# A two-layer diffusion backbone: another order of its stages, and norm gains applied where rows are loaded

## The chip, the cores and the metric

The kernel runs on one core of one Trainium2 chip. The metric is the device time of one execution, in microseconds (us); less is better. The engines of the core are TensorE (PE in the profile; PEld is its weight load), VectorE (DVE), ScalarE (ACT), GpSimd (POOL) and SyncE (SP), which here issues nearly all DMAs, in the order in which they stand in its program. Each engine works through its own instructions in order and waits on semaphores for the others.

## The reference

1024 latent tokens and 256 context tokens of width 1024 go through two layers. Each layer has an attention mixer and a feed-forward network (FFN) with a convolution over three tokens; both are modulated by a condition vector and followed by a LayerNorm of a scaled residual sum. Context tokens leave the trunk after layer 0, and only the latent tokens are returned.

```python
for l in range(DEPTH):                      # DEPTH = 2
    ctx_out = l < DEPTH - 1
    m_lat = split(silu(c) @ ada_w[l] + ada_b[l], 6)      # modulation rows 0..5
    m_ctx = split(silu(c_ctx) @ ada_w[l] + ada_b[l], 6)
    h_lat = modulate(x_lat, m_lat[0], m_lat[1])          # x * (1 + scale) + shift
    h_ctx = modulate(x_ctx, m_ctx[0], m_ctx[1])
    y_lat, y_ctx = mixer[l](h_lat, h_ctx)   # projection, attention, output projection
    x_lat = layer_norm(DN_ALPHA * x_lat + m_lat[2] * y_lat, ln_g[l, 0], ln_b[l, 0])
    f_lat = conv_ffn(modulate(x_lat, m_lat[3], m_lat[4]), ...)
    x_lat = layer_norm(DN_ALPHA * x_lat + m_lat[5] * f_lat, ln_g[l, 1], ln_b[l, 1])
    if ctx_out:
        x_ctx = layer_norm(DN_ALPHA * x_ctx + m_ctx[2] * y_ctx, ln_g[l, 0], ln_b[l, 0])
        f_ctx = conv_ffn(modulate(x_ctx, m_ctx[3], m_ctx[4]), ...)
        x_ctx = layer_norm(DN_ALPHA * x_ctx + m_ctx[5] * f_ctx, ln_g[l, 1], ln_b[l, 1])
return x_lat

def conv_ffn(h, w_up, conv_w, conv_b, w_down):           # D_FF = 2816
    u = h @ w_up
    acc = conv_b + sum(shifted(u, j) * conv_w[j] for j in range(3))
    a, g = split(acc, 2)
    return (silu(g) * a) @ w_down
```

## The kernel before, in words

Everything is float32 in and out. A product is made as three matmuls on values split into a high and a low part (lines L308, L309, L310). ScalarE makes the high part (L99), and VectorE or GpSimd subtracts it for the low part (L100); a weight thus takes a load of 512 KB into a buffer "raw", two conversions on ScalarE and two subtractions. Order on each engine is the order in which the program text issues the instructions; there is no planner. A buffer name with few copies makes the next user wait for the last reader of the copy that it takes over.

The stages run in this order, with the stretch of the profiled execution that each takes, in us:

- 0 to 392: modulation vectors of layer 0, transposes of the input, first projection.
- 392 to 800: attention of layer 0 (global heads and neighbourhood heads).
- 800 to 952: first output projection, `l0_out`. `out_project` walks over groups of row tiles of 128 tokens: latent tiles 0 and 1 as a pair, 2 to 7 singly, context tiles 8 and 9 as a pair. For each tile it loads the attention output in two halves (yr), splits them (yh on ScalarE, L1074; yl on GpSimd, L1075), multiplies (PSUM tile o), adds the gated residual row tile x, normalizes (`ln`: statistics on VectorE, two small instructions L269 and L270 on GpSimd, and the scaling L271 on VectorE), and hands the tile before to `finish`. `finish` transposes a latent tile on TensorE (PSUM tile tr, L285) into the FFN's input h2 (L302, L303), multiplies by the norm's gain and adds its bias on GpSimd (`gain_bias`, L275 and L276, with the broadcast rows lg and lb), and stores it. A context tile is stored twice: normalized only (DRAM tensor xnm) and with gain and bias (x1c).
- 952 to about 1760: latent FFN of layer 0, up to 1797 with the input build of the context FFN.
- 1797 to 1994: context FFN of layer 0 (`lean`: 256 tokens).
- 1994 to 2160: second projection, `l1_project`. 2160 to 2388: attention of layer 1.
- 2388 to 2530: second output projection, `l1_out`, whose pairs are tiles 0, 1 and 6, 7.
- 2530 to 3283: FFN of layer 1.

An FFN (`ffn`) runs over 11 groups. A group loads two up weights (wa, wg), makes four up products of 128 x 1024 (PSUM tag u, two buffers), convolves each (ScalarE L1229, then VectorE L1232 and L1236, result cv), multiplies pairs of them (L1246) and splits the product into gT. Between its two halves stand the down products of the group before: eight row tiles, each 12 matmuls into a PSUM tile d (two buffers), added by VectorE to the accumulator "a" of the tile (L1266). A tile of d thus waits until VectorE has reached the "a" two tiles earlier, and a third u waits until the first has been convolved. GpSimd multiplies the down weights by the gate row (L1211) and splits weights (L100). At the start the residual rows are loaded straight into the accumulators: `nc.sync.dma_start(a, xsrc(t))`.

The rest of the modulation vectors (parts 2 to 5 of layer 1, latent tokens) are made beside the latent FFN of layer 0, as `ada_items`: 16 items, each a block of 1024 x 256 of the weight matrix, loaded in two halves of 512 KB through the one buffer araw and summed on VectorE by eight instructions of 128 x 256 into "acc" (L201 for the first, L205 for the others). Four items stand in each of four groups, and each item's "acc" goes to the DRAM tensor adp. During the context FFN `ada_reduce` loads these sums back and lets TensorE sum them over the partitions. The rows are turned into modulation columns m2 (after the latent FFN's last group) and m3 (after that of the context FFN).

After the latent FFN the last down products are normalized (`finish_l`), transposed into the second projection's input h1, and stored as xn2. Then the context rows xc are loaded back from xnm and transposed into h2c. In `l1_project` the normalized latent rows are loaded once more (x2t), given gain and bias on GpSimd between the rope products q (L364), and stored as x2, from where `l1_out` takes its residual rows. `l1_out` gives its own result gain and bias in `finish` and stores x3, which the last FFN loads.

## Time and profile before

| What | Value |
|---|---|
| median of 3 runs | 3276.53 us (3273.34 to 3279.7) |
| profiled execution, its own time | 3284.98 us |
| span of the profiled execution | 3283.2 us |
| granted TensorE clock over the span | 0.953 |
| TensorE busy | 2997.3 us (91%), 17084 matmuls |
| weight loads busy | 2407.3 us (73%) |
| VectorE busy | 1797.4 us (55%), 3037 instructions |
| ScalarE busy | 1120.1 us (34%), 2072 instructions |
| GpSimd busy | 1278.7 us (39%), 1158 instructions |
| DMA | 102 GB/s mean; 264.32 MB read, 66.39 MB written |
| GpSimd, weight split L100 | 276 of 1378 ns |
| VectorE, accumulator sum L1266 | 172 of 1217 ns |

The profile is one execution, seen from the hardware. A line of it names the source line, the engine, the operation, and output and inputs by the program's names; an arrow behind a number names the instruction that ended the idle time before it. TensorE's clock is granted by a throttle: 1.00 is full speed, and 0.50 makes each matmul take twice as long.

### The profile page before, as it was taken

The numbers are of one execution on the slowest core, as the hardware profiler recorded it, in microseconds if no ns is written. First come the engines' busy times: TensorE is split into PE (matmuls) and PEld (weight loads), VectorE is DVE, ScalarE is ACT, GpSimd is POOL, SyncE is SP. The second block draws the span as 40 slices with busy tenths as digits, with TensorE's granted clock in tenths as the row PEclk, the third lists the DMA queues.
The fourth block names the chain that finished last, engine by engine and source line by source line (L and its number), as shares of the span: only waits on it lengthen the run. The fifth ranks groups of instructions, "written<-read, shape, count | busy, mean of one in ns | idle before, by whom it ended". The sixth has DMA issues, their size and how long they took to land. (4 is left out here: it accounts for less than half of the span.)

```text
span 3283.2 us, 44502 instructions
## 1 busy us (share of the span) xinstructions
PE 2997.3 (91%) x17084; PEld 2407.3 (73%) x17084; DVE 1797.4 (55%) x3037; ACT 1120.1 (34%) x2072; POOL 1278.7 (39%) x1158
## 2 busy tenths in 40 slices
PE   6889889998888889999996998889977999999997
PEld 2768777776766778888875897767765888888885
DVE  3687676664786663334337784267745333343336
ACT  2222255565222212222225662257722222222220
POOL 3641043353553223322315444635557333223323
PEclk7999999999998999999997998889998999999999
DMA  7366721043344331111114654642143111111111
GB/s 231 117 181 215 225 80 38 10 144 98 96 136 145 114 117 60 52 39 39 58 33 164 190 180 152 195 136 63 33 132 132 61 57 46 39 46 58 52 39 64
DMA packets 252801, 333.61 MB, mean 102 GB/s; under 512 B 19322, under 2 KB 196970, under 8 KB 251050
## 3 DMA queue, kind: packets, MB, share of 16 engines
q1 hardware_dynamic: 252588, 330.77, 32.0%
q8 instruction: 134, 2.20, 0.3%
q14 instruction: 79, 0.65, 0.1%
HBM read 264.32 MB, written 66.39 MB: 101 GB/s over the span
## 5 line engine op out<-in xcount | busy, mean ns | idle before, releaser
L100 POOL TENSOR_TENSOR w<-raw,w 128x512 fp32r<-128x512 f32 x276 | 377.3, 1378 | 719.3 <-ACT w L99 666.9
L99 ACT CAST w<-raw 128x512 fp32r<-128x512 f32 x452 | 272.8, 620 | 642.4 <-PE u L310 272.4
L1232 DVE SCALAR_TENSOR_TENSOR cv<-u,cc,cv 128x1023 f32<-128x1023 f32 (+1 forms) x132 | 133.8, 1013 | 613.7 <-ACT cv L1229 613.5
L622 POOL TENSOR_SCALAR P<-P,rin 128x640 f32<-128x640 f32 (+3 forms) x288 | 250.8, 875 | 350.7 <-DVE rin L621 319.0
L308 PE MATMUL d<-w,gT 128*128 128x512 f32 x792 | 314.4, 397 | 37.1 <-DVE a L1266 21.9
L310 PE MATMUL d<-w,gT 128*128 128x512 f32 x792 | 313.2, 396 | 3.5 <-POOL gT L1249 3.5
L309 PE MATMUL d<-w,gT 128*128 128x512 f32 x792 | 313.2, 395 | 0.0
L1249 POOL TENSOR_TENSOR gT<-cv,gT 128x1024 fp32r<-128x1024 f32 (+1 forms) x66 | 122.9, 1863 | 480.5 <-ACT gT L1248 478.8
L308 PE MATMUL u<-h2lh,w 128*128 128x512 f32 x704 | 280.5, 398 | 10.4 <-DVE cv L1236 6.7
L309 PE MATMUL u<-h2ll,w 128*128 128x512 f32 x704 | 280.3, 398 | 2.7 <-DVE h2ll L300 2.7
L310 PE MATMUL u<-h2lh,w 128*128 128x512 f32 x704 | 280.0, 398 | 0.0
L308 PE MATMUL u<-h3lh,w 128*128 128x512 f32 x704 | 278.5, 396 | 0.0
L310 PE MATMUL u<-h3lh,w 128*128 128x512 f32 x704 | 278.2, 395 | 0.0
L309 PE MATMUL u<-h3ll,w 128*128 128x512 f32 x704 | 278.2, 395 | 0.0
L1266 DVE TENSOR_TENSOR a<-a,d 128x1024 f32<-128x1024 f32 x172 | 209.3, 1217 | 125.0 <-PE d L310 124.0
L1229 ACT ACTIVATE cv<-u,cc,cc 128x1024 f32<-128x1024 f32 (+1 forms) x132 | 131.1, 993 | 379.8 <-PE u L310 378.8
L205 DVE SCALAR_TENSOR_TENSOR acc<-araw,cs,acc 128x512 f32<-128x512 f32 (+1 forms) x280 | 211.2, 785 | 36.9 <-DMA araw<-in_ada_w_dram 33.3
L598 PE MATMUL S<-k,q 64*128 64x256 f32 (+2 forms) x1824 | 192.7, 341 | 15.6 <-DVE nm L1444 4.5
L308 PEld LDWEIGHTS d<-w,gT 128*128 128x128 f32 x792 | 151.4, 191 | 73.2 <-DVE a L1266 24.1
L619 ACT ACTIVATE P<-P,nm 128x641 f32<-128x641 f32 (+4 forms) x208 | 161.4, 777 | 89.5 <-DVE nm L1444 50.7
L310 PEld LDWEIGHTS d<-w,gT 128*128 128x128 f32 x792 | 151.3, 191 | 37.5 <-POOL gT L1249 5.2
L309 PEld LDWEIGHTS d<-w,gT 128*128 128x128 f32 x792 | 151.4, 191 | 30.9
(212 smaller groups left out, 6538.5 us busy)
## 6 DMA issues: line engine op xcount, KB each, us to landing
raw<-in_up_dram SPq DMA_DIRECT2D x132, 512.0 KB
araw<-in_ada_w_dram SPq DMA_DIRECT2D x80, 512.0 KB
raw<-in_down_dram SPq DMA_DIRECT2D x66, 512.0 KB
raw<-in_w_in_dram SPq DMA_DIRECT2D x28, 512.0 KB
x<-x SPq DMA_DIRECT2D x24, 512.0 KB
yr<-yT SPq DMA_DIRECT2D x36, 256.0 KB
wt<-in_ada_w_dram SPq DMA_DIRECT2D x16, 512.0 KB
x<-in_x_dram SPq DMA_DIRECT2D x16, 512.0 KB
```

The source lines that it names most:

```text
L99: nc.scalar.copy(hi, s)
L100: (lo_eng or nc.vector).tensor_sub(lo, s, f32(hi))
L205: nc.vector.scalar_tensor_tensor(acc[v], r[:, k - k0], sc, acc[v], ALU.mult, ALU.add)
L308: nc.tensor.matmul(ps, lh, rh, start=first, stop=False)
L309: nc.tensor.matmul(ps, lh, rl, start=False, stop=False)
L310: nc.tensor.matmul(ps, ll, rh, start=False, stop=last)
L598: self.nc.tensor.matmul(outs[a], q[r, x, qs], k[r, y, ks], start=(i == 0), stop=(i == 2))
L619: nc.scalar.activation(P[:, :m], P[:, :m], AF.Exp, bias=negm, scale=-1.0, accum_out=den)
L622: nc.gpsimd.tensor_scalar(P[:, :n], P[:, :n], rin, 1.0, ALU.mult, ALU.mult)
L1229: nc.scalar.activation(cv, ps, AF.Identity, bias=cc[3][:, f : f + 1], scale=cc[1][:, f : f + 1])
L1232: nc.vector.scalar_tensor_tensor(cv[:, 1:T], ps[:, 0 : T - 1], cc[0][:, f : f + 1], cv[:, 1:T], ALU.mult, ALU.add,)
L1266: nc.vector.tensor_add(acc[t], acc[t], pf)
```

## The change

1. **Order of stages.** The first output projection takes the context tiles 8 and 9 first and builds their FFN input h2c at once (xnm and xc go). The context FFN follows, then the latent FFN, then the second projection. m2 is made at the end of the first projection, m3 in the second projection.
2. **Gain and bias where rows are loaded.** `finish` of both output projections and the second projection no longer calls `gain_bias`. An FFN gets the norm's rows and applies them after loading (`rows`): a product and a sum of 128 x 1024 on VectorE for each row tile, sixteen instructions at the start of a latent FFN (L1222, L1223 of the changed kernel), and in the context FFN two for each tile in its last down products. The two norm rows are broadcast first, in a latent FFN into a gT buffer. The latent FFN's result is stored once, normalized, as x2; the second output projection applies gain and bias on GpSimd to each residual tile as it comes in (`prep`), ahead of that tile's yl.
3. **First FFN weights.** The first up weights of an FFN are loaded and split between the last two tiles of the output projection ahead of it (`after`, `early`); half of the low parts go to VectorE. In the context FFN the second up weights go into raw buffers that begin where `l0_out`'s tiles (hst among them) lay; SP reaches their load behind the store of tile 7, the gate row and the two norm rows.
4. **Pairs.** Latent tiles 0 and 1 of the first output projection, and tiles 6 and 7 of the second, become single tiles. The first gate row is loaded ahead of the tiles.
5. **Modulation items.** Two items in each of eight groups of the latent FFN. Each item is summed over the partitions at once, in a d buffer (two matmuls L224, L225 of 128 x 256); adp and `ada_reduce` are out of use.
6. **Last sums.** The last attention outputs are stored from ScalarE's queue instead of SP's (`queue`, and j == 3).

```diff
@@ out_project
+        gate_of(groups[0][0])
+        self.t(st, [128, D], "x", bufs=4)
+        self.t(st, [128, 512], "hst", bufs=2)
...
                         nc.sync.dma_start(tl[t][3], xsrc(t))
+                        if prep is not None:
+                            prep(tl[t][3])
...
                 done = (t, x)
+        if after is not None:
+            after()
         finish(*done)
@@ l0_out
-                    nc.sync.dma_start(d["xnm"][o, :], xn)
+                    hi, lo = (v[:, :, o] for v in h2c)
+                    self.build_hT(st, pt, xn, self.m1[1], hi, lo)
                     dst = d["x1c"][o, :]
-                self.gain_bias(xn, xn, gr, br)
                 nc.sync.dma_start(dst, xn)
             self.out_project(
-                io["w_out0"], d["yT0"], [[0, 1]] + [[t] for t in range(2, 8)] + [[8, 9]],
+                io["w_out0"], d["yT0"], [[8, 9]] + [[t] for t in range(8)],
                 xsrc, gate_of, finish, st, wx, pp,
+                after=lambda: self.early.extend(self.load_up(0, 0, self.raw, True)),
             )
@@ ffn
-            side = side(cvp, e2) if side else self.ada_items(cvp, None, jobs)
+            side = self.ada_items(
+                cvp, lambda: self.t(pd, [128, 2, 512], "d")[:, 0], jobs
+            )
...
-                if not lean:
-                    nc.sync.dma_start(a, xsrc(t))
...
+                gb = f32(self.t(st, [128, 2, T], "gT", R, bufs=4 if final else 3))
+            for i in range(2):
+                self.bcast(gb[:, i], norm[i])
+            def rows(t, x):
+                nc.sync.dma_start(x, xsrc(t))
+                nc.vector.tensor_mul(x, x, gb[:, 0])
+                nc.vector.tensor_add(x, x, gb[:, 1])
+            if not lean:
+                for t in range(nt):
+                    rows(t, acc[t])
...
+                if c0 == 0 and early:
+                    return early
+                return self.load_up(l, c0, raw, lean)
...
-                for _ in range(-(-12 * len(jobs) // (ng - 1)) or 3):
+                for _ in range(-(-24 * len(jobs) // (ng - 1))):
                     next(side, None)
@@ l1_project
-                nc.sync.dma_start(x, d["xn2"][t * 128 : (t + 1) * 128, :])
-                self.gain_bias(x, x, g2, b2)
-                nc.sync.dma_start(o, x)
...
-                    if h0 == 0:
-                        residual(t)
@@ l1_out
-                self.gain_bias(xn, xn, gr, br)
                 nc.sync.dma_start(rows("x3")(t), xn)
             self.out_project(
-                io["w_out1"], d["yT1"], [[0, 1]] + [[t] for t in range(2, 6)] + [[6, 7]],
+                io["w_out1"], d["yT1"], [[0, 1]] + [[t] for t in range(2, 8)],
                 rows("x2"), lambda t: gate, finish, st, wx, pp,
+                lambda x: self.gain_bias(x, x, gr, br),
+                lambda: self.early.extend(self.load_up(1, 0, self.raw, True)),
             )
@@ run (order of the calls)
-  l0_out(h2l); ffn(latent, jobs); build h2c from xnm; ffn(context, side=ada_reduce); l1_project
+  l0_out(h2l, h2c); ffn(context, early); ffn(latent, jobs); l1_project
```

VectorE in the latent FFN, in a group with modulation items, from the items ahead of the first convolution of the next group's first half to the first accumulator. acc is the sum of an item, cv a convolution, u an up product, a an accumulator, d a down product. Before:

```order
L205 SCALAR_TENSOR_TENSOR acc_2332_12319<-araw_12326,cs_123,acc_2332_12319 128x256
L201 TENSOR_SCALAR acc_2371_12717<-araw_12718,cs_123 128x256
L205 SCALAR_TENSOR_TENSOR acc_2371_12717<-araw_12718,cs_123,acc_2371_12717 128x256 x3
L1232 SCALAR_TENSOR_TENSOR cv_10807<-u_10758,cc_136_474,cv_10807 128x1023
L1236 SCALAR_TENSOR_TENSOR cv_10807<-u_10758,cc_139_481,cv_10807 128x1023
L205 SCALAR_TENSOR_TENSOR acc_2371_12717<-araw_12724,cs_123,acc_2371_12717 128x256 x4
L201 TENSOR_SCALAR acc_2410_13115<-araw_13116,cs_123 128x256
L205 SCALAR_TENSOR_TENSOR acc_2410_13115<-araw_13116,cs_123,acc_2410_13115 128x256 x2
L1232 SCALAR_TENSOR_TENSOR cv_10860<-u_10811,cc_136_474,cv_10860 128x1023
L205 SCALAR_TENSOR_TENSOR acc_2410_13115<-araw_13116,cs_123,acc_2410_13115 128x256
L1236 SCALAR_TENSOR_TENSOR cv_10860<-u_10811,cc_139_481,cv_10860 128x1023
L1266 TENSOR_TENSOR a_2094_10011<-a_2094_10011,d_10869 128x1024
```
The same stretch after the change (L1261 and L1265 are the convolution, L1275 the product of two, L1295 the accumulator):

```order
L1275 TENSOR_TENSOR cv_13440<-cv_13440,cv_13493 128x1024
L205 SCALAR_TENSOR_TENSOR acc_2647_13973<-araw_13974,cs_121,acc_2647_13973 128x256 x2
L205 SCALAR_TENSOR_TENSOR acc_2647_13973<-araw_13980,cs_121,acc_2647_13973 128x256 x4
L1261 SCALAR_TENSOR_TENSOR cv_13647<-u_13598,cc_134_472,cv_13647 128x1023
L1265 SCALAR_TENSOR_TENSOR cv_13647<-u_13598,cc_137_479,cv_13647 128x1023
L201 TENSOR_SCALAR acc_2689_14380<-araw_14381,cs_121 128x256
L205 SCALAR_TENSOR_TENSOR acc_2689_14380<-araw_14381,cs_121,acc_2689_14380 128x256 x3
L205 SCALAR_TENSOR_TENSOR acc_2689_14380<-araw_14387,cs_121,acc_2689_14380 128x256 x4
L1261 SCALAR_TENSOR_TENSOR cv_13700<-u_13651,cc_134_472,cv_13700 128x1023
L1265 SCALAR_TENSOR_TENSOR cv_13700<-u_13651,cc_137_479,cv_13700 128x1023
L1295 TENSOR_TENSOR a_2467_12360<-a_2467_12360,d_13709 128x1024
```
Ahead of the accumulator stand, before and after, the end of one half item, three further halves and the two convolutions; after the change the first two halves stand together ahead of the first convolution.

VectorE at the start of the last FFN. h3lh is the FFN's input, w and raw are weights. Before, the first convolution follows the input's last conversion:

```order
L271 TENSOR_SCALAR x_22754<-x_22754,mv_22915,rs_22917 128x1024
L302 CAST h3lh_22067<-hst_22953 128x4x128
L302 CAST h3lh_22067<-hst_22965 128x4x128
L1232 SCALAR_TENSOR_TENSOR cv_23093<-u_23044,cc_142_488,cv_23093 128x1023
L1236 SCALAR_TENSOR_TENSOR cv_23093<-u_23044,cc_145_495,cv_23093 128x1023
L100 TENSOR_TENSOR w_23269<-raw_23266,w_23269 128x512
```
After the change, the last rows ahead of the first convolution; gT_23006 holds the norm's rows:

```order
L1222 TENSOR_TENSOR a_4320_23000<-a_4320_23000,gT_23006 128x1024
L1222 TENSOR_TENSOR a_4319_22999<-a_4319_22999,gT_23006 128x1024
L1223 TENSOR_TENSOR a_4320_23000<-a_4320_23000,gT_23006 128x1024
L1223 TENSOR_TENSOR a_4319_22999<-a_4319_22999,gT_23006 128x1024
L1222 TENSOR_TENSOR a_4318_22998<-a_4318_22998,gT_23006 128x1024
L1261 SCALAR_TENSOR_TENSOR cv_23098<-u_23049,cc_140_486,cv_23098 128x1023
L1223 TENSOR_TENSOR a_4318_22998<-a_4318_22998,gT_23006 128x1024
L1265 SCALAR_TENSOR_TENSOR cv_23098<-u_23049,cc_143_493,cv_23098 128x1023
L1261 SCALAR_TENSOR_TENSOR cv_23151<-u_23102,cc_140_486,cv_23151 128x1023
L1265 SCALAR_TENSOR_TENSOR cv_23151<-u_23102,cc_143_493,cv_23151 128x1023
```
Fifteen of the sixteen row operations stand ahead of the first half of the first convolution, the last one inside it.

GpSimd in the second projection, after the input is built. q is a rope product, x2t the residual row tile, g and b the norm's rows. Before:

```order
L364 TENSOR_TENSOR q_17350<-rp_3045_17351,rp_3046_17352 128x512
L275 TENSOR_TENSOR x2t_17357<-x2t_17357,g_3028_17287 128x1024
L276 TENSOR_TENSOR x2t_17357<-x2t_17357,b_3029_17288 128x1024
L364 TENSOR_TENSOR q_17387<-rp_3050_17388,rp_3051_17389 128x512
L364 TENSOR_TENSOR q_17424<-rp_3055_17425,rp_3056_17426 128x512
L364 TENSOR_TENSOR q_17471<-rp_3062_17472,rp_3063_17473 128x512
```
After:

```order
L364 TENSOR_TENSOR q_17355<-rp_3047_17356,rp_3048_17357 128x512
L364 TENSOR_TENSOR q_17387<-rp_3051_17388,rp_3052_17389 128x512
L364 TENSOR_TENSOR q_17419<-rp_3055_17420,rp_3056_17421 128x512
L364 TENSOR_TENSOR q_17461<-rp_3061_17462,rp_3062_17463 128x512
L364 TENSOR_TENSOR q_17503<-rp_3067_17504,rp_3068_17505 128x512
```
The products q follow one another, and the row work on x2t is gone. It comes back at the start of the second output projection, on GpSimd too, where x is the residual tile, lg and lb are the norm's rows, and yl is the low part of the attention output:

```order
L275 TENSOR_TENSOR x_22140<-x_22140,lg_22067 128x1024
L276 TENSOR_TENSOR x_22140<-x_22140,lb_22068 128x1024
L1085 TENSOR_TENSOR yl_22138<-yr_22144,yh_22137 128x512
L275 TENSOR_TENSOR x_22151<-x_22151,lg_22067 128x1024
L276 TENSOR_TENSOR x_22151<-x_22151,lb_22068 128x1024
L1085 TENSOR_TENSOR yl_22149<-yr_22155,yh_22148 128x512
```
Before, only the rows on yl stood there.

TensorE at the end of the latent FFN. tr is a transpose of a finished tile a, mm a product of the second projection, h1lh and h1ll its input. Before, the last down product is followed by transposes alone (xc is a context row tile):

```order
L310 MATMUL d_14707<-w_14319,gT_14301 128x512
L285 MATMUL tr_14634<-ident_58,a_2098_10019 128x128 x4
L285 MATMUL tr_14646<-ident_58,a_2098_10019 128x128 x4
L285 MATMUL tr_14682<-ident_58,a_2099_10021 128x128 x4
L285 MATMUL tr_14694<-ident_58,a_2099_10021 128x128 x4
L285 MATMUL tr_14730<-ident_58,a_2100_10023 128x128 x4
L285 MATMUL tr_14742<-ident_58,a_2100_10023 128x128 x4
L285 MATMUL tr_14764<-ident_58,a_2101_10025 128x128 x4
L285 MATMUL tr_14776<-ident_58,a_2101_10025 128x128 x4
L285 MATMUL tr_14808<-ident_58,xc_14806 128x128 x4
L285 MATMUL tr_14820<-ident_58,xc_14806 128x128 x4
L285 MATMUL tr_14834<-ident_58,xc_14832 128x128 x4
```
After:

```order
L310 MATMUL d_17184<-w_16865,gT_16847 128x512
L285 MATMUL tr_17111<-ident_58,a_2463_12356 128x128 x4
L285 MATMUL tr_17123<-ident_58,a_2463_12356 128x128 x4
L308 MATMUL mm_17330<-w_17300,h1lh_16874 128x512
L309 MATMUL mm_17330<-w_17300,h1lh_16874 128x512
L310 MATMUL mm_17330<-w_17300,h1ll_16875 128x512
L308 MATMUL mm_17330<-w_17303,h1lh_16874 128x512
L285 MATMUL tr_17159<-ident_58,a_2462_12355 128x128 x4
L309 MATMUL mm_17330<-w_17303,h1lh_16874 128x512
L285 MATMUL tr_17171<-ident_58,a_2462_12355 128x128 x4
```
Products of the second projection stand among the last two tiles' transposes, and the context tiles are no longer there.

More of the change, by code (lines that the diff above doesn't have):

```diff
@@ L1465, in values @@
                             "(a p) t -> p a t", p=128
-                        ), sp,
+                        ), sp, nc.scalar if kv and t >= 6 else nc.sync,
                     )
@@ L1549, in run @@
+        self.ffn(0, TLAT, h2l, hl, rows("x1"), a[0, 0, 5], begin_l, finish_l, norm=norm,
                  jobs=[(1, p, (0,)) for p in (2, 3, 4, 5)])
[L1551 to L1559 removed]
```

144 lines of the change are left out of this document (59 added, 85 removed).

## The prediction

> **What bounds the kernel now.** I read the table by stage first, then the engine waits, then single stretches. Columns of the first fence: stretch in us, its length, busy time and instructions of TensorE, of its weight loads, VectorE, ScalarE and GpSimd, the granted TensorE clock, the DMA share and GB/s.
>
> ```profile
> 800.00:952.00 152.00, 127.00 (x552) 101.58 (x552) 108.54 (x182) 39.23 (x93) 79.19 (x59) 0.92 0.43 115
> 952.00:1040.00 88.00, 77.84 (x299) 60.39 (x300) 58.38 (x75) 19.69 (x25) 42.42 (x25) 0.90 0.52 178
> 1040.00:1232.00 192.00, 165.61 (x684) 132.85 (x683) 127.00 (x156) 36.92 (x46) 43.44 (x25) 0.92 0.36 110
> 1232.00:1716.00 484.00, 484.00 (x2094) 391.62 (x2093) 178.22 (x156) 115.14 (x141) 138.77 (x84) 1.00 0.15 47
> 1716.00:1797.00 81.00, 46.65 (x206) 36.58 (x205) 56.97 (x81) 39.59 (x97) 41.90 (x41) 0.73 0.41 137
> 1797.00:1994.00 197.00, 188.72 (x1310) 174.21 (x1308) 151.73 (x225) 121.50 (x227) 88.49 (x72) 0.99 0.56 177
> 1994.00:2160.00 166.00, 141.03 (x728) 119.81 (x727) 63.93 (x134) 33.00 (x76) 83.82 (x62) 0.89 0.59 185
> 2388.00:2530.00 142.00, 103.60 (x456) 83.27 (x457) 68.73 (x83) 38.68 (x91) 96.10 (x70) 0.88 0.34 116
> 868.70:872.10 3.40, 3.40 (x12) 2.90 (x11) 3.40 (x3) 0.00 (x0) 3.40 (x3) 0.50 0.63 154
> ```
>
> TensorE is the bound: in the clean part of an FFN (1232 to 1716) it never idles, at 484/2094 = 0.231 us a matmul. To be had is what the other stages lose: idle time, and half of the busy time at clock 0.5. Idle time is length minus busy: 25 (first output projection), 10 (start of the latent FFN), 26 (its groups with modulation work), 34 (its end and the start of the context FFN), 8, 25 (second projection), 38 (second output projection). The clock adds between half and all of (1-clock) x length, since part of the slow time is idle.
>
> The waits: first two rows, 1040 to 1232; three, 1716 to 1797; one, 1994 to 2160; two, 2388 to 2530; two, 800 to 952. Then single instructions of TensorE (start, us, name, idle time before it and who ended it).
>
> ```profile
> PE d L308 <- DVE a L1266: 19.2, 2, 10.0
> PE d L308 <- DVE a L1270: 7.2, 1, 7.2
> ...
> PE tr L285 <- DVE a L271: 12.5, 6, 3.9
> PE tr L285 <- DMA xc<-xnm: 6.0, 1, 6.0
> PE u L308 <- DVE h2ch L302: 3.9, 1, 3.9
> ...
> PE tr L385 <- POOL q L364: 14.4, 6, 4.3
> ...
> PE tr L285 <- DVE x L271: 27.6, 6, 11.1
> PE o L308 <- ACT yh L1074: 9.9, 1, 9.9
> ...
> PE tr L285 <- DVE x L271: 11.0, 6, 3.0
> PE o L308 <- ACT yh L1074: 10.7, 1, 10.7
> ```
>
> ```profile
> 868.26 1.55 PE L285 MATMUL tr<-ident,x 128*128 128x128 f32 x8 [1.96 <-DVE x L271]
> 1129.60 0.79 PE L308 MATMUL d<-w,gT 128*128 128x512 f32 x1 [9.25 <-DVE a L1266]
> 1208.90 0.79 PE L308 MATMUL d<-w,gT 128*128 128x512 f32 x1 [9.96 <-DVE a L1266]
> 2513.45 0.87 PE L285 MATMUL tr<-ident,x 128*128 128x128 f32 x3 [11.09 <-DVE x L271]
> 2525.07 1.30 PE L285 MATMUL tr<-ident,x 128*128 128x128 f32 x5 [9.69 <-DVE x L271]
> ```
>
> Behind the 1.96 us at 868.26 comes the last row of the table: 3.4 us at clock 0.50, 1.7 us lost. So a short wait costs nearly double.
>
> **The change, stage by stage.** The durations: VectorE in a group with modulation work, in order, then groups of like instructions (the mean in ns stands behind the busy time) of 952 to 1232 (L205, first L1246), 1240 to 1700 (the next five) and 1994 to 2160 (the last).
>
> ```profile
> 1099.17 1.28 DVE L1232 SCALAR_TENSOR_TENSOR cv<-u,cc,cv 128x1023 f32<-128x1023 f32 x1
> ...
> 1112.24 0.35 DVE L201 TENSOR_SCALAR acc<-araw,cs 128x256 f32<-128x256 f32 x1 [4.27 <-DMA araw<-in_ada_w_dram]
> 1112.63 1.53 DVE L205 SCALAR_TENSOR_TENSOR acc<-araw,cs,acc 128x256 f32<-128x256 f32 x3
> ...
> 1117.82 2.05 DVE L205 SCALAR_TENSOR_TENSOR acc<-araw,cs,acc 128x256 f32<-128x256 f32 x4 [1.15 <-DMA araw<-in_ada_w_dram]
> ...
> 1128.33 1.21 DVE L1266 TENSOR_TENSOR a<-a,d 128x1024 f32<-128x1024 f32 x1
> ```
>
> ```profile
> L205 DVE SCALAR_TENSOR_TENSOR acc<-araw,cs,acc 128x256 f32<-128x256 f32 x112 | 79.8, 712 | 22.6 <-DMA araw<-in_ada_w_dram 19.4
> ...
> L1246 DVE TENSOR_TENSOR cv<-cv,cv 128x1024 f32<-128x1024 f32 x7 | 10.8, 1538 | 3.8 <-ACT cv L1245 3.6
> ...
> L1246 DVE TENSOR_TENSOR cv<-cv,cv 128x1024 f32<-128x1024 f32 x14 | 19.0, 1360 | 8.7 <-ACT cv L1245 8.3
> ...
> L99 ACT CAST w<-raw 128x512 fp32r<-128x512 f32 x81 | 50.1, 619 | 182.9 <-PE u L310 95.1 <-PE d L310 87.0
> L1229 ACT ACTIVATE cv<-u,cc,cc 128x1024 f32<-128x1024 f32 x27 | 32.6, 1208 | 106.0 <-PE u L310 106.0
> ...
> L100 POOL TENSOR_TENSOR w<-raw,w 128x512 fp32r<-128x512 f32 x53 | 68.4, 1290 | 170.2 <-ACT w L99 167.3
> L1211 POOL TENSOR_TENSOR raw<-raw,gate 128x1024 f32<-128x1024 f32 x14 | 33.6, 2397 | 10.0 <-DMA raw<-in_down_dram 6.5 <-DVE cv L1246 3.5
> ...
> L275 POOL TENSOR_TENSOR x2t<-x2t,g 128x1024 f32<-128x1024 f32 x8 | 19.1, 2390 | 19.6 <-DMA x2t<-xn 19.6
> ```
>
> Gains are positive; brackets are bounds.
>
> *First output projection, +14 (0 to +20).* Its first product waits 10.7 us for yh, whose load stands behind two row broadcasts. These go, and the last sums leave on ScalarE's queue. A 512 KB load that VectorE awaits costs 4.27 us, so two save 0 to 8.5; I take 5. The GpSimd passes L275 and L276, 2.39 us each, also go; I take 9 of the 11.0 us of normalization waits and the slow clock behind them.
>
> *Start of both FFNs of layer 0, -10 (-25 to +6).* Now 10 idle and 4 to 9 of slow clock, 17. The context FFN will start behind tile 7: its second up weights reuse space that tile 7's last split still reads, and their load stands behind that tile's store, the gate and two broadcasts on SP. Split (some 4), load (4.27), conversion (0.62 on ScalarE, 1.29 on GpSimd): about 11 idle and 3 of clock. At the latent start sixteen row operations stand on VectorE ahead of the second convolution. At 1.36 (L1246, a product of this size) they take 22 us, from when the rows land, by estimate 24 us after the last context product; two convolutions follow, and the next up product wants to run at 39: 10 idle, 3 of clock.
>
> *Modulation items, +3 (-14 to +34).* An item costs two loads through one buffer, and VectorE, which works in order, stands still for each: 4.27, or 1.15 where a convolution stands between. After the change a group gets two items instead of four, in eight groups instead of four; in six of them four half items and two convolutions stand, as now, between the convolution that ends a group's second half (1099.17) and the first "a" that frees a bank (1128.33). Counted from the last product of that half: convolution 1.21+2x1.28, split, first half item and gate product, to 8.3; then three half items of 2.0, each behind a load of about 4, a convolution (2.6) beside one of these loads: 14, 20, 26; last convolution and "a", 30.1. TensorE wants the bank after two up products (48x0.231 each) and two down tiles (12x0.231 each), at 28.2: idle 1.9 us, and 4.3 where L205 takes its mean 0.712 instead of 0.51. From the other side: VectorE now comes some 5.4 us late to 1099.17, and without that 9.25 becomes 3.9. I take 3.4, and 1.7 for the clock: 6x5.1 = 31, against 26.4 idle and 8 of clock now. Bounds: no wait (+34), or six times 8 (-14).
>
> A page bears on the 1.7. The Trainium skill, "TensorE: Matmul & The Clock Gate", Part 1, says that the clock is halved after an idle window of about 3.4 us; the row at 868.26 shows it halved behind 1.96. By the page most of these six waits would cost no clock, and the sum would be up to 10 us better.
>
> *Context FFN, +3 (-3 to +8).* Its eight modulation sums leave; part of its 8 idle us returns with the latent FFN's sums.
>
> *Latent end, +22 (8 to 32).* Now 34 idle and 11 of clock. The context transposes and their load (6.0, 3.9) move, and the second projection's products stand among the last transposes. Left: the start-up chain of the last down product (6), some 8 of the 12.5 of normalization, 8 of clock.
>
> *Second projection, +27 (10 to 36).* The 14.4 us behind q are GpSimd's: L275 and L276 on x2t, eight tiles, move to the output projection. The stage loses 25 idle and some 12 of clock; I leave 10.
>
> *Second output projection, +11 (-3 to +22).* At its start L275 and L276 on x now stand on GpSimd ahead of each of the first four yl: 4 (load) + 4.8 + 1.3 = 10 before the products flow, then 0.6 each for the next three: -2. At its end the pair 6, 7 (11.09 and 9.69 idle, 4 of clock) becomes single tiles: tile 6 is ready under tile 7's products; tile 7 waits some 8 us (its chain, with eight weight splits L100 in its way), 4 of clock: +13.
>
> *Start of the last FFN, -9 (-15 to 0).* It loses nothing now. Sixteen row operations precede the first convolution: from about 13 us after the transposes (gate broadcast, two L1211, four splits), 15x1.36 = 20, convolution 2.6: 37, against 29 when the third up product wants its bank: 8 idle, 1 of clock. *Attention start*, modulation columns made earlier: -1 (-3 to 0).
>
> Sum: 14-10+3+3+22+27+11-9-1 = 60. The profiled execution took 3284.98, 8.5 above the median 3276.53; against it the sum gives 3225, against the median 3216, which I predict.
>
> **The rivals.**
> - *The items fit.* If loads land a little sooner the six waits vanish: 3216-31 = 3185. For it: 1.9 us is little. Against it: L205's mean of 0.712.
> - *A group with items costs what it does now.* 1208.90-1129.60 = 79.3 against 288x0.231 = 66.6: 12.7 a group. In all eight groups 102 instead of 31: 3287, slower. It decides from 12.2 a group. For it: same buffer, same order on VectorE. Against it: half the items.
> - *The stage ends wait for something else.* At the latent end and in the second projection VectorE or the loads become what GpSimd was, and half of 22+27 is lost: 3240.
> - *The row operations are held up.* Each of the two sets of sixteen waits behind one L100: 16x1.29 = 21 more at each place, 3258. For it: L1246 is 1.54 beside modulation work and 1.36 without. Against it: that is 0.18, not 1.29. The Trainium skill, "SBUF — State Buffer", Who interferes with whom, has the rule: a VectorE instruction with two SBUF inputs shares a port with GpSimd, and whoever comes later waits in full.
> - *No effect*, 3276: the waits named are not what holds the stages. The stage table speaks against it.
>
> **How the numbers follow.** Forecast (3195 to 3240) 0.53; items fit 0.15; ends wait 0.15; row operations 0.06; slower 0.08; no effect 0.03. The range 3168 to 3262 leaves out the last two and a little at each end, 0.15. The three times spread over 0.2%, and less can't be told from no change: faster 0.89, same 0.03, slower 0.08.
>
> **What would show it.** Right: no wait of tr for q on GpSimd; no load xc<-xnm; in six latent groups one wait of d for "a" of 2 to 5 us; one wait of some 8 us for x at the second output projection's end; a wait of u for its bank, 8 to 10 us, in the first group of the latent and of the last FFN; about 10 us idle ahead of the context FFN. Wrong: latent groups of 79 us, or a first o that waits over 12 us.

## The result, and the profile after

The changed kernel takes 3239.66 us (median of 4 runs, 3235.94 to 3243.53), against 3274.94 us before (4 runs, 3266.17 to 3279.70). The ratio is 0.9895, with a 95% interval of 0.9870 to 0.9921: about 34 us faster. The forecast was 3216 with a range of 3168 to 3262; the sign and the range held, and some two fifths of the forecast gain (60 us) are missing. The profiled execution after took 3243.53 us (span 3241.8 us, granted clock 0.960), 41 us less than the profiled one before.

The first fence is the table by stage of the changed kernel, with the columns of the prediction's first fence. The stages are, in order: first output projection; start of the context FFN; its rest; start of the latent FFN; its groups with modulation items; its clean groups; its end; second projection; second output projection; start of the last FFN.

```profile
800.60:938.20 137.60, 126.27 (x586) 104.19 (x584) 82.62 (x197) 43.20 (x102) 44.25 (x46) 0.95 0.49 131
938.20:990.00 51.80, 35.55 (x238) 33.89 (x238) 36.31 (x66) 28.56 (x56) 20.05 (x14) 0.80 0.76 243
990.00:1135.00 145.00, 143.75 (x1016) 133.80 (x1015) 119.67 (x169) 91.81 (x171) 58.41 (x51) 1.00 0.54 168
1135.00:1215.00 80.00, 60.90 (x250) 47.91 (x249) 61.33 (x68) 18.54 (x29) 27.68 (x22) 0.87 0.50 171
1215.00:1625.00 410.00, 387.55 (x1627) 310.69 (x1626) 217.74 (x249) 91.87 (x118) 112.79 (x66) 0.97 0.24 75
1625.00:1922.00 297.00, 297.00 (x1288) 240.24 (x1287) 119.03 (x113) 75.76 (x97) 88.77 (x56) 1.00 0.17 53
1922.00:1969.00 47.00, 33.54 (x142) 26.30 (x141) 33.12 (x49) 19.29 (x48) 23.87 (x26) 0.83 0.24 88
1969.00:2110.00 141.00, 131.88 (x738) 112.90 (x737) 56.04 (x128) 38.78 (x95) 53.34 (x52) 0.98 0.47 139
2340.20:2474.70 134.50, 101.70 (x450) 82.30 (x449) 62.39 (x81) 35.09 (x82) 95.11 (x68) 0.90 0.37 128
2474.70:2520.00 45.30, 37.17 (x142) 29.37 (x142) 29.46 (x27) 12.15 (x20) 11.95 (x8) 0.85 0.44 155
```

Length minus busy is TensorE's idle time. It fell from 25 to 11 us in the first output projection, from 25 to 9 in the second projection, and from 34 to 14 at the latent end. New idle time stands at three starts: 16 (context FFN), 19 (latent FFN), 8 (last FFN), where before there were 10 at the latent start, 8 over the whole context FFN and none at the last. The groups with items have 22, as much as the 26 of before.

What TensorE waited for between 800 and 2520 us (us in total, times, longest):

```profile
PE u L308 <- DVE cv L1265: 25.2, 11, 12.7
PE tr L285 <- DVE x L271: 21.1, 6, 10.0
PE d L308 <- DVE a L1295: 18.0, 5, 4.2
PE o L308 <- ACT yh L1084: 16.1, 2, 10.4
PE u L308 <- ACT w L99: 12.4, 1, 12.4
...
PE tr L385 <- POOL q L364: 6.7, 3, 4.0
PE o L310 <- POOL yl L1085: 6.6, 2, 3.6
...
PE d L308 <- DVE a L1299: 4.4, 1, 4.4
```

And the single instructions at the starts, one of the items' waits, and the last tile of the second output projection:

```profile
950.60 0.58 PE L308 MATMUL u<-h2ch,w 128*128 128x256 f32 x1 [12.38 <-ACT w L99]
1196.68 0.76 PE L308 MATMUL u<-h2lh,w 128*128 128x512 f32 x1 [12.70 <-DVE cv L1265]
1318.70 0.79 PE L308 MATMUL d<-w,gT 128*128 128x512 f32 x1 [3.40 <-DVE a L1295]
2473.18 1.94 PE L285 MATMUL tr<-ident,x 128*128 128x128 f32 x8 [9.99 <-DVE x L271]
2507.22 0.77 PE L308 MATMUL u<-h3lh,w 128*128 128x512 f32 x1 [8.13 <-DVE cv L1265]
```

The wait for q on GpSimd fell from 14.4 to 6.7 us, the load of xc is gone, and the item groups wait six times for an accumulator (18.0 in five, 4.4 once). The row operations took their price at both latent starts (12.70 and 8.13), and the context FFN waits 12.38 us for its second up weights.

### The profile page after: what moved, and what is told of

The parts are those of the page before. It is cut to its first block, busy times and chain, and to the rows that moved or that the text cites. A ratio compares the mean times of both kernels' runs of the same rounds, so it can differ in the third digit from the quotient of the medians.

```text
span 3241.8 us, 44441 instructions
## 1 busy us (share of the span) xinstructions
PE 2984.2 (92%) x17100; PEld 2401.5 (74%) x17100; DVE 1792.3 (55%) x3091; ACT 1122.8 (35%) x2080; POOL 1180.8 (36%) x1120
## 4 chain that ended last, share of the span: by engine, by line
PE 68%; DVE 13%; DMA 7%; POOL 4%; ACT 3%; issue 3%; SPq 1%; POOLq 0%; ACTq 0%; DVEq 0%
PE u L308 9%; PE u L310 9%; PE u L309 9%; PE d L308 5%; PE d L310 5%; PE d L309 5%; PE S L602 4%; PE pv L747 3%; PE T L733 3%; DVE acc L205 3%; PE mm L310 3%; PE mm L308 3%; PE mm L309 3%; DMA araw<-in_ada_w_dram 3%; PE T L698 2%
## 5 line engine op out<-in xcount | busy, mean ns | idle before, releaser
L100 POOL TENSOR_TENSOR w<-raw,w 128x512 fp32r<-128x512 f32 x274 | 368.4, 1353 | 745.5 <-ACT w L99 701.2
L1261 DVE SCALAR_TENSOR_TENSOR cv<-u,cc,cv 128x1023 f32<-128x1023 f32 (+1 forms) x132 | 133.7, 1013 | 538.1 <-ACT cv L1258 538.1
L308 PE MATMUL u<-h2lh,w 128*128 128x512 f32 x704 | 278.7, 396 | 12.7 <-DVE cv L1265 12.7
L1295 DVE TENSOR_TENSOR a<-a,d 128x1024 f32<-128x1024 f32 x172 | 209.3, 1217 | 140.4 <-PE d L310 139.5
L205 DVE SCALAR_TENSOR_TENSOR acc<-araw,cs,acc 128x512 f32<-128x512 f32 (+1 forms) x280 | 205.2, 763 | 71.7 <-DMA araw<-in_ada_w_dram 68.0
```

The costliest lines, as they stand in the source:

```text
L100: (lo_eng or nc.vector).tensor_sub(lo, s, f32(hi))
L205: nc.vector.scalar_tensor_tensor(acc[v], r[:, k - k0], sc, acc[v], ALU.mult, ALU.add)
L308: nc.tensor.matmul(ps, lh, rh, start=first, stop=False)
L1261: nc.vector.scalar_tensor_tensor(cv[:, 1:T], ps[:, 0 : T - 1], cc[0][:, f : f + 1], cv[:, 1:T], ALU.mult, ALU.add,)
L1295: nc.vector.tensor_add(acc[t], acc[t], pf)
```

## Experiments

All are edits of the changed kernel unless said otherwise. Ratios are to the kernel before, with 95% intervals; the changed kernel stands at 0.9895.

**Row operations behind the first group's products.**

```diff
-            if not lean:
-                for t in range(nt):
-                    rows(t, acc[t])
...
                 g0 = up_pair(wa, wg, f, 0)
+                some(4)          # rows() of the next four tiles
...
                 g1 = up_pair(wa, wg, f + 1, 1)
+                some(4)
```

> The sixteen row operations of the latent FFNs are issued behind the first group's products instead of ahead of them; on VectorE two to four of them now stand ahead of the second (latent FFN) or first (last FFN) convolution, not fifteen or sixteen. Theory (the row operations in VectorE's queue hold the bank that the third up product wants): the waits of 12.70 us in the latent FFN and 8.13 us in the last FFN fall under 3 us, the slow clock behind them goes too, and the kernel gains 18 to 30 us on the changed kernel (to 3210 to 3222). Rival (the backlog on VectorE only moves on): the same time comes back as waits for the first accumulators or the third convolution, and the gain is under 6 us.

Ratio 0.9855 (0.9838 to 0.9871), 3225.76 us. The last FFN's wait is gone. In the latent FFN the wait for the convolution is gone too, but another stands in its place. First what TensorE waits for there, then VectorE and SyncE's queue:

```profile
PE u L308 <- ACT w L99: 8.3, 1, 8.3
...
PE u L310 <- POOL w L100: 2.9, 2, 2.6
```

```profile
1193.59 1.21 DVE L1221 TENSOR_TENSOR a<-a,gT 128x1024 f32<-128x1024 f32 x1
1194.72 0.68 DVE L100 TENSOR_TENSOR w<-raw,w 128x512 fp32r<-128x512 f32 x1
```

```profile
1195.55 0.38 SPq L1180 DMA_DIRECT2D raw<-in_up_dram  x1
```

A split L100 of the down weights stands behind row operations on VectorE; the load of the second group's weights goes out 0.15 us after that split ends, and TensorE's next up product waits for it. So each theory had one place. The last FFN, from its first up product to the end, is 10.8 us shorter (756.2 against 767.0; six other profiles that leave it as it is show 766.0 to 767.2): there the cost is real and recovered. In the latent FFN most of it moves on. From its first up product to the first of the second projection it takes 815.8 us against 821.4, but seven profiles with the changed kernel's order of instructions there lie between 812.9 and 822.7, so no gain is shown. The gain of the kernel, about 13 us, lies under the 18 to 30 expected.

**Row operations behind those splits as well.** `some(8)` stands behind `load_down` instead.

> As rows_late, but the row operations stand on VectorE behind the four splits L100 of the first down weights as well. Theory (in rows_late one such split stood behind the row operations, held its raw buffer, and so held the load of the second group's up weights on SyncE: waits of 8.34 and 2.56 us for w): these waits fall under 2 us together, and the time is 8 to 14 us under that of rows_late. Rival (the load of the weights is late for another reason, or the next waits take over): w's waits stay above 5 us or the time is within 4 us of rows_late.

Ratio 0.9822 (0.9804 to 0.9841), 3221.23 us. The waits for w went to 0.6 us, but the sum of an item now waits (ahl is its split, made when VectorE has the sum ready):

```profile
PE d L224 <- ACT ahl L220: 11.1, 1, 11.1
...
PE u L308 <- DVE cv L1271: 2.4, 1, 2.4
```

The theory of the held buffer is right, the gain is not: VectorE's backlog held up the next thing in its queue. From the first latent up product to the first product of the second projection it is 814.3 us here and 815.8 in rows_late; the medians differ by 4.5 us. The ratios differ by more (the runs of before in the two sets are 6 us apart), so the size of that gain stays unclear; by the medians it is of the rival's size (within 4 us), by the ratios, some 11 us, of the theory's (8 to 14).

**Items in quarters through three buffers.**

```diff
-            side = self.ada_items(cvp, bank, jobs)
+            side = self.ada_items(cvp, bank, jobs, nraw=3, G=2)   # 4 loads of 256 KB per item
...
-                for _ in range(-(-24 * len(jobs) // (ng - 1))):
+                for _ in range(-(-35 * len(jobs) // (ng - 1))):   # still two items a group
```

> Modulation items are loaded in quarters of 256 KB through three buffers instead of halves of 512 KB through one; still two items in each of eight groups, the same sums on VectorE. Theory (VectorE stands still for a load through the one buffer, and is so late for the accumulator): the six waits of 3.4 to 4.5 us for an accumulator fall under 1 us each, and the stretch of the item groups gains 20 to 35 us. Rival (VectorE's own work, slowed beside GpSimd's weight passes, is what is late): the waits stay above 2.5 us each and the gain is under 8 us.

Ratio 0.9783 (0.9769 to 0.9798), 3202.31 us: some 37 us, the largest single gain here. The latent FFN, counted as above, takes 782.2 instead of 821.4 us, 39 less where 20 to 35 were expected. The six waits are gone (the longest left for an accumulator is 0.3 us). First the row of the item groups in the table by stage, then VectorE's sums in the item groups, changed kernel above, this kernel below:

```profile
1203.00:1590.00 387.00, 386.67 (x1681) 312.60 (x1680) 230.24 (x250) 97.69 (x126) 118.15 (x68) 1.00 0.27 82
```

```profile
L205 DVE SCALAR_TENSOR_TENSOR acc<-araw,cs,acc 128x256 f32<-128x256 f32 x91 | 57.6, 633 | 47.3 <-DMA araw<-in_ada_w_dram 44.8
```

```profile
L205 DVE SCALAR_TENSOR_TENSOR acc<-araw,cs,acc 128x256 f32<-128x256 f32 x95 | 76.8, 808 | 11.3 <-DMA araw<-in_ada_w_dram 9.0
```

VectorE's wait for araw fell from 44.8 to 9.0 us. Its sums even became slower (808 against 633 ns), and TensorE still lost only 0.33 us in 387. The order on VectorE shifted a little too, but in the group of the 3.40 us wait the work ahead of the first accumulator is the same in both kernels: fourteen L205 and two L201, counted from the convolution that ends the group before (1288.19 in the changed kernel, 1271.50 here), with 8.6 us of waits for araw in the changed kernel and 2.6 here. So the load through the single buffer was the cause and VectorE's own pace was not. The edit changes the size of the pieces and the number of buffers together; which of the two does it is not shown.

**The residual rows' gain and bias on VectorE.**

```diff
-                lambda x: self.gain_bias(x, x, gr, br),
+                lambda x: (nc.vector.tensor_mul(x, x, gr), nc.vector.tensor_add(x, x, br)),
```

> Gain and bias of the residual rows in the second output projection are made on VectorE instead of GpSimd. Theory (yl stands behind L275 and L276 on GpSimd): the waits of 3.60 and 3.04 us for yl at the start go, the first o (10.44 us, behind its load) stays, and the gain is 4 to 9 us. Rival (the loads of yr, which stand behind the broadcasts and rows in the DMA queue, are what is late): yl's waits become waits for yh of the same size, and the gain is under 2 us.

Ratio 0.9863 (0.9847 to 0.9879), 3226.76 us, some 10 us faster. TensorE's waits in the second output projection:

```profile
PE tr L285 <- DVE x L271: 12.9, 2, 10.0
PE o L308 <- ACT yh L1084: 9.9, 1, 9.9
PE o L310 <- POOL yl L1085: 0.9, 1, 0.9
```

The wait for yl fell from 6.6 to 0.9 us and that for x from 15.6 (four times) to 12.9 (twice); from the first o to the first product of the last FFN it is 114.1 us instead of 124.1. The last tile's 10.0 stays.

**The residual work back in the second projection** (x2t, L275 and L276 as before the change, with the result stored for the second output projection).

> One part undone: the residual rows' gain and bias go back into the second projection, on GpSimd between the rope products, and are stored for the second output projection. Theory (this work is what the transposes of q waited for): the second projection loses 18 to 28 us, and the start of the second output projection gains 6 to 10 us, so the kernel is 8 to 20 us slower than the changed kernel. Rival (the new order of the stages took those waits away): the second projection loses under 8 us, and the kernel is no slower or a little faster.

Ratio 0.9907 (0.9879 to 0.9935), 3241.47 us. TensorE's wait for q, from the first product of the second projection on:

```profile
PE tr L385 <- POOL q L364: 16.0, 6, 9.3
PE tr L385 <- DVE qst L373: 4.4, 2, 2.6
```

The wait is back (16.0 us in six, 14.4 before the change). From the stage's first product mm to the first S that waits in the attention it is 174.2 us against 153.5: the 20.7 us lie inside the 18 to 28. The second output projection takes 113.5 instead of 124.1, 10.6 less. Together that is 10 us; the median moved by 2 and the ratio by 0.12%, inside the intervals. In this profile the latent FFN, which the edit leaves alone, was 8.5 us shorter: its instructions stood in the same order and TensorE was idle for as long (51.0 us, 51.2 in the changed kernel), but it was busy for only 27.7 us at clock 0.50 instead of 46.8, which is 9.5 us of loss less. At its places the theory holds; the total doesn't show it.

**The first FFN weights not early** (`after` left out in both output projections).

> One part undone: the first up weights of the context FFN and of the last FFN are loaded where the FFN begins in the text, not between the last two tiles. Theory: in the last FFN they cost something, because their conversions on ScalarE and GpSimd stand ahead of tile 7's normalization: the wait of 9.99 us for x falls to 6 to 8 us; in the context FFN they save something, since without them all four loads go to the late buffers: the wait there grows by 3 to 8 us. Net within 6 us. Rival (the wait for x is tile 7's own chain): it stays at 9 to 11 us.

Ratio 0.9909 (0.9886 to 0.9932), 3246.11 us. Both of my sizes were wrong: the wait for x stayed at 10.13 us, so it is the last tile's own chain, and the context FFN lost nothing. There TensorE waits 15.1 us for w in place of 12.4, but its first product starts later, and from the first o to the first latent up product it is 334.9 against 334.0 us. Kernels with the same order of instructions as the changed one there show 328.0 to 334.0 us, so no gain of the early first weights is shown.

**The context FFN's second up weights early too.**

```diff
-                after=lambda: self.early.extend(self.load_up(0, 0, self.raw, True)),
+                after=lambda: self.early.extend(
+                    [self.load_up(0, c, self.raw, True) for c in (0, DFF)]),
```

> The second up weights of the context FFN's first group are loaded and split early too, through the two raw buffers that are free during the output projection, instead of through the context FFN's own buffers. Theory (the 12.38 us wait at the context start is made by the space that tile 7's split still reads, and by the three broadcasts that stand ahead of the load): the wait falls under 4 us, and the kernel gains 8 to 16 us on the changed kernel. Rival (the conversions on ScalarE and GpSimd are what is late, or the down weights and the second group's weights, which stay in the late buffers, take the wait over): the first wait goes but another of 5 us or more stands within the next 15 us, and the gain is under 5 us.

Ratio 0.9889 (0.9874 to 0.9905), 3234.68 us. The 12.38 us became 0.5 for w, but tile 7's normalization (2.33 us before) now takes 5.0 and the splits 2.9:

```profile
PE tr L285 <- DVE x L271: 5.0, 1, 5.0
PE u L308 <- DVE cv L1266: 3.0, 3, 1.7
PE u L310 <- POOL w L100: 2.7, 3, 1.4
PE u L308 <- ACT w L99: 0.5, 1, 0.5
```

From the first o to the first latent up product it is 328.9 us, 5.1 less than the changed kernel. That shows no gain: the kernel with items in quarters, whose instructions there stand in the changed kernel's order, took 328.0. The time is not clear of the intervals either, so the 8 to 16 us expected are not there, and the rival of the next wait describes the result better.

**The context FFN's broadcasts behind the weights.** The gate and the two norm rows are broadcast after the first group's products instead of ahead of its weights.

> In the context FFN the gate row and the two norm rows are broadcast behind the second up weights' loads instead of ahead of them; the weights still use the FFN's own buffers. If the three broadcasts (order on SyncE and the shared transfer) make the wait of 12.38 us, it falls under 5 us. If the space that tile 7's split still reads makes it, it stays above 8 us, since the load is still issued at the end of that split. Theory: both have a share, the transfer shrinks from 7.9 to about 4 us, and the wait is 8 to 9 us; the time changes by 2 to 6 us.

Ratio 0.9882 (0.9866 to 0.9899), 3240.40 us. The wait fell to 7.42 us. The load is issued 5.05 us behind tile 7's store (937.72 after 932.67), as in the changed kernel (942.00 after 937.03), so the space holds it as before; but the first half is there after 3.75 us (conversion at 941.47) instead of 7.93 (949.93). The two causes share the wait: 5 us are the broadcasts, 7 the space and the load itself. Of the 5 us, 3.4 came back as waits for splits (L100), and from the first o to the first latent up product it is 333.6 us against 334.0: no gain is shown.

**Last sums stored from SyncE's queue.**

> One part undone: the last attention outputs are stored from SyncE's queue again. Theory (the two broadcasts that are gone from the first output projection shortened its first wait from 10.68 to 5.67 us, not the queue): the wait stays under 7 us, that of the second output projection stays at 10 to 11 us, and the time is the same within 0.2%. Rival (the queue gave it): the first wait is back at 9 to 11 us, and the kernel is 3 to 6 us slower.

Ratio 0.9900 (0.9876 to 0.9923), 3241.58 us. The first o waits 6.69 us (5.67 with ScalarE's queue, 10.68 before the change), that of the second output projection 10.41. By these single profiles one of the five microseconds is the queue's. The other four go with what else changed ahead of the first o: the two broadcasts are gone and the first tiles are others. No run here separates these two.

**Four edits together**: items in quarters, residual rows on VectorE, both context weights early, rows behind the splits.

> Four edits together: the items' quarters through three buffers, the residual rows' gain and bias of the second output projection on VectorE, the context FFN's second up weights early, and the row operations behind the first group (now issued behind the splits of the first down weights, so that on VectorE these splits stand ahead of them). If the four costs are separate, their gains add up: six waits for an accumulator, the waits for yl, most of 12.38, 12.70 and 8.13 us go, and the time is 3165 to 3185. If they share a cause or hide one another, it stays above 3190.

Ratio 0.9711 (0.9692 to 0.9731), 3178.94 us, 60 us under the changed kernel and inside the 3165 to 3185 expected if the costs are separate. By their ratios the separate gains were 37, 10, 2 and 24 us, 73 in all (the last is that of the rows behind the splits, the form used here). So most of it adds up; whether the other 13 us are lost to shared causes the intervals leave open. In the latent FFN TensorE now waits 8.5 us for ahl and 3.7 us for an accumulator.

**And the items begin in the second group.**

```diff
-                for _ in range(-(-35 * len(jobs) // (ng - 1))):
+                for _ in range(-(-35 * len(jobs) // (ng - 1)) if j else 0):
```

> As combined, and the modulation items begin in the second group instead of the first, two in each of eight groups. Theory (in the first group the row operations and the items share VectorE, and this made combined's waits of 8.51 us for ahl and 3.70 us for an accumulator): both go, with the slow clock behind them, and the time is 8 to 16 us under combined's. Rival (the items take the same waits with them to the next groups): within 4 us of combined.

Ratio 0.9667 (0.9651 to 0.9684), 3168.90 us: 10 us under combined (14 by the ratios), where 8 to 16 were expected, and the best version, 3.3% under the kernel before. The wait for ahl (8.5 us in combined) and the one for an accumulator are gone, with 6.8 us for the convolution in their place, and the item groups run without a gap:

```profile
PE u L308 <- DVE cv L1272: 6.8, 1, 6.8
```

```profile
1215.00:1590.00 375.00, 375.00 (x1632) 303.41 (x1630) 212.54 (x227) 94.54 (x122) 109.88 (x65) 1.00 0.25 75
```

## Why the prediction held, and where the rest of the gain went

Loss is idle time plus half of the busy time at clock 0.50, counted over every TensorE instruction of the two profiled executions.

| Term | Forecast | Loss before | Loss after | Gain |
|---|---|---|---|---|
| first output projection | +14 | 32.9 | 16.2 | +17 |
| starts of both layer-0 FFNs and context FFN | -10 +3 | 17.3 + 12.2 | 20.7 + 1.2 + 24.7 | -17 |
| modulation items | +3 | 34.3 | 35.0 | -1 |
| latent end | +22 | 43.2 | 19.9 | +23 |
| second projection | +27 | 37.2 | 11.3 | +26 |
| second output projection | +11 | 44.0 | 39.0 | +5 |
| start of the last FFN | -9 | 0.0 | 12.7 | -13 |
| start, first projection, attention of both layers | -1 | 134.2 | 135.9 | -2 |

The sum is 38 of the span's 41 us, against 60 forecast.

- *Right in place and size:* the first output projection, the latent end and the second projection, 66 us of gain measured against 63. Putting the residual work back brought the wait for q back: it was GpSimd's, as the prediction had it, and the rival that the stage ends wait for something else is out. Its 3240 us came true for other reasons. One sign did not come: TensorE still waits 6.7 us for q. At the longest of these waits (4.05 us) five weight splits L100 stand ahead of that q on GpSimd, four from 2017.61 on (5.05 us) and one at 2024.46, while q itself runs at 2025.69; the prediction had left 10 us in the stage without saying for what.
- *Starts of the layer-0 FFNs, mis-sized by 10 us with the context FFN.* The two waits were 12.38 us for 11 and 12.70 for 10 (4 us more). The slow clock behind them was as forecast: 5.50 and 5.22 us at 0.50 (rows below) cost 2.8 and 2.6 us, where I put 3 each. The term that was too small is what I left for the rest: 9 us for the context FFN, where the short waits beside the two cost 16 us. They are 11.5 us of waits (3.15 for a convolution, 3.07 for gT, 2.00 for an item's sum, and smaller ones) and 4.7 us of clock behind two of them.
- *Start of the last FFN, -13 for -9.* The wait was 8.13 us for a forecast of 8. (The forecast's own terms, 13, 20 and 2.6, make 36 and not 37, so 7.) The clock behind it cost 2.7 us (5.38 us at 0.50), for which I had put 1; another 1.9 us counted in this row is the slow clock behind the 9.99 us wait ahead of the stage.

```profile
950.60:956.10 5.50, 5.50 (x25) 5.49 (x26) 4.04 (x5) 3.36 (x6) 3.05 (x2) 0.50 0.60 207
1196.68:1201.90 5.22, 5.22 (x12) 4.10 (x13) 5.22 (x7) 2.05 (x2) 1.80 (x1) 0.50 0.19 52
2507.22:2512.60 5.38, 5.38 (x13) 4.22 (x14) 2.88 (x3) 2.34 (x2) 0.00 (x0) 0.50 0.00 0
```

- *Second output projection, +5 for +11.* The end went as forecast: the pair's 11.09 and 9.69 became one wait of 9.99. The start did not. I charged GpSimd's two passes ahead of the first yl and then 0.6 us a tile. The passes for the next tile stand between one yl and the next, so that a yl comes every 6 us (rows below), and TensorE waited 3.60 and 3.04 us more. VectorE doing them gave 10 us.

```profile
2354.18 1.26 POOL L1085 TENSOR_TENSOR yl<-yr,yh 128x512 fp32r<-128x512 f32 x1
2355.40 2.37 POOL L275 TENSOR_TENSOR x<-x,lg 128x1024 f32<-128x1024 f32 x1
2357.85 2.34 POOL L276 TENSOR_TENSOR x<-x,lb 128x1024 f32<-128x1024 f32 x1
2360.15 1.26 POOL L1085 TENSOR_TENSOR yl<-yr,yh 128x512 fp32r<-128x512 f32 x1
```

- *Modulation items, -1 for +3.* Six waits, at 3.36 to 4.45 us where I took 3.4, and 12.5 us of clock where I took 10. The step that failed is the side of VectorE's pace: I took the mean of L205 to decide between 1.9 and 4.3 us. It was 633 ns, between my two, and the run with three buffers shows that the loads set the wait whatever the pace. (120 matmuls of 0.231 us are 27.7 and not 28.2, so the smaller of the two was 2.4 by its own terms.)
- *The row operations held up by GpSimd:* no. The sixteen ran at 1.21 us each at both places, below the 1.36 I took, with no stop between them. Just ahead of them, beside L1240 on GpSimd, four L205 took 4.06 us (2.05 at 1312.96, with GpSimd idle) and one L221 2.07. That agrees with the rule of the Trainium skill named there ("SBUF — State Buffer", Who interferes with whom), but GpSimd had nothing to do while the rows ran, so this kernel did not put the rival to a test.
- *The clock.* The page "TensorE: Matmul & The Clock Gate" of the Trainium skill, Part 1, would have spared short waits. The trace after doesn't follow it: waits of 2.34 and 2.00 us are followed by 3.40 us at half clock each, and all six waits for an accumulator had slow clock behind them, 1.4 to 3.0 us of loss each. Nor is it sure that a short wait costs this much, as the prediction had it from one row: behind a wait of 2.92 us at 2391.41 the clock stayed at 1.00, and so it did in the run with three buffers behind the same wait of 2.34 us for "a" (1901.55 there). What decides between the two is not shown.

```profile
1949.23 1.80 PE L285 MATMUL tr<-ident,a 128*128 128x128 f32 x8 [2.34 <-DVE a L271]
...
2391.41 1.09 PE L285 MATMUL tr<-ident,x 128*128 128x128 f32 x8 [2.92 <-DVE x L271]
...
2412.43 1.06 PE L285 MATMUL tr<-ident,x 128*128 128x128 f32 x8 [2.00 <-DVE x L271]
```

```profile
1949.40:1952.80 3.40, 3.40 (x13) 3.01 (x13) 2.89 (x6) 2.36 (x7) 1.76 (x2) 0.50 0.37 154
2391.41:2396.00 4.59, 4.59 (x25) 3.94 (x25) 2.78 (x6) 2.90 (x8) 1.67 (x3) 1.00 0.48 171
2413.60:2417.00 3.40, 3.40 (x10) 2.63 (x9) 2.98 (x3) 0.02 (x1) 3.40 (x3) 0.50 0.23 96
```

One statement ahead of the prediction is wrong: the order on an engine is not always that of the program text. In the text all sixteen row operations stand ahead of the first convolution; in VectorE's rows of the last FFN the last one stands inside it, and in the latent FFN the first convolution (1162.63) stands ahead of all sixteen (from 1174.71 on). So the text alone doesn't settle the order, and an edit's effect is to be read from the engines' rows.

What stays open: the last tile's wait of 10 us in the second output projection, which no edit here moved, and the last 7 us of the latent start.

## What to carry to other kernels

Work that moves off a late path goes somewhere, and its new price is set by the queue it joins: sixteen cheap operations on VectorE, and two passes on GpSimd for each tile, gave back some 13 and 10 us of the gain because something urgent stood behind them. When an in-order engine streams weights through one buffer, look first at its idle time before those instructions, not at their duration; smaller pieces through more buffers gave as much here as the whole reordering. Charge a new wait of TensorE with the slow clock behind it, but not in proportion to its length: behind 12.38, 12.70, 9.99 and 8.13 us it cost 2.6 to 2.8 us each here, behind the six waits of 3.36 to 4.45 us 2.1 on average, and behind 2 to 3 us 1.7 or nothing. A single profile can be off by this alone (9.5 us in one latent FFN above), so compare a stage with the other profiles that leave it as it is.

## What the runs showed of the hardware that was not expected

- A wait of 2 us can be followed by 3.40 us at half of TensorE's clock, and one of 2.92 us by none (above). Waits of 12.38 and 12.70 us were followed by 5.50 and 5.22 us at 0.50, no more than the 2.9 to 6.1 us behind the six waits of 3.36 to 4.45.
- With three broadcasts of a row over 128 partitions issued ahead of it, a 512 KB load took 7.93 us from issue to conversion; with them issued behind it, 3.75.
- VectorE's sums L205 slowed from 633 to 808 ns when they no longer waited for their loads, with no cost to TensorE.
